# A three-part change in the first projection of a diffusion block: inverse roots by `pow`, later transposes, four modulation vectors made there

## The chip, the cores and the metric

The kernel runs on one core of a Trainium2 chip. The metric is the device time of one execution in microseconds (us). The engines of the core are TensorE (PE; its weight loads are PEld), VectorE (DVE), ScalarE (ACT), GpSimd (POOL) and SyncE (SP), which here only issues DMAs.

## The reference, cut to what matters

Two layers of a transformer with adaptive normalisation run over 256 latent and 256 context tokens of width 1024, all in float32. Each layer has six modulation vectors, `silu(cond) @ ada_w + ada_b`, cut into six parts of 1024 (numbered 0 to 5 here): shift, scale and gate of the mixer, then of the FFN. The first layer is attention plus a convolution and a plain FFN, the second an S5 state-space mixer and a mixture of eight experts.

```
sh1, sc1, g1, sh2, sc2, g2 = adaln(c, ada_w[l], ada_b[l])
h = modulate(rmsnorm(x, norm1_g[l]), sh1, sc1)
q, k, v, a, g = split(h @ w_in)             # 1024 -> 5 x 512
q, k = rmsnorm(heads(q), q_g), rmsnorm(heads(k), k_g)      # per head of 64
u = a * sigmoid(g); u = conv31(u)           # depthwise over tokens
y = concat(attention(q, k, v), silu(layernorm(u))) @ w_out
x = x + g1 * y
x = x + g2 * ffn(modulate(rmsnorm(x, norm2_g[l]), sh2, sc2))
```

`rmsnorm` of q and k needs, for each of 512 tokens and 8 heads, `1 / sqrt(mean of squares + 1e-6)`: 128 partitions by 32 numbers for q, as many for k.

## The kernel before, in words

**Matrix products.** Each float32 weight tile of 128x2048 (1 MB) is loaded into one of four ring buffers `raw`, then split (`split`, L190) into a rounded part `wh` (ScalarE, L203) and a rest `wl` (VectorE, or GpSimd for the names in `ON_POOL`, L205). `mm3` (L221) makes three matmuls of 128x128 by 128x512 for each product (L223 to L225). Splitting a tile frees its ring buffer, and `Stream.issue` then issues the next load. The order of all loads is written out in `plan` (L238) and goes through SP's queue in that order.

**First projection** (`mix_in`, L577). Five outputs n of 512 columns are made in the order 3, 4, 0, 1, 2: conv input a, gate g, q, k, v. Each takes two weight tiles (`kh` 0 and 1), each tile four steps k, each step four token tiles t: 48 matmuls a tile. When q's two tiles are done, ScalarE squares the four accumulators (L655), VectorE sums per head (L656), `rsqrt` (L494) makes the inverse roots by a bit trick and three Newton steps on VectorE, and VectorE writes the normalised `qn` (L658) from the accumulators in PSUM. `rest` is what TensorE then has to do for the last output (for n = 4 the transposes `glu` of a times gate, L592; for q and k the transposes `turn_qk`, L601, whose results ScalarE copies, L602); it is called inside the next output's loop, so those transposes stand between its matmuls.

**Convolution.** After `glu`, 31 taps for each of four channel blocks go into lists (`conv`, L662): VectorE does three blocks (L676), GpSimd one (add, L686, of a product that ScalarE makes, L685, in two buffers). `pump` (L227) takes a few taps of each list per step k (`MIXV`, `MIXP`); what is left goes into the attention.

**Modulation vectors.** The first two of layer 0 are made at the start. Each of the others is four units (`ada_unit`, L364): one 1 MB tile of `ada_w` and four products `ada_mm` (L333) with a 32-column weight, put on four column groups of TensorE. Two units are one half; ScalarE copies its accumulator out (`ada_out`, L371) and issues a store of rows (for vectors 2 to 5 of layer 1 to `partd`, `ada_to_dram`, L430). The units wait in a list in the order of the `ada_queue` calls in `layer0`; `ada_step` (L465) takes up to n of them, if their loads have been issued. Before the change the list begins with layer 0's vectors 2, 3 and 4, taken in the attention (L813), then 0's 5 and 1's 0 to 5, taken two at a time in the FFN loop (L964) and in its tail (`tail`, L854, `TAIL`). `partd` is read at the start of the S5 stage (L1246).

**Order.** Instructions of the engines listed in `ORDERED` are kept in the order of the program; for "mix" (the first projection) these are ScalarE, GpSimd and SP. TensorE and VectorE are ordered there by the compiler's scheduler. PSUM has eight banks of 128x512, all under one tag (L180).

**Later stages.** Attention, output projection, FFN, S5 and at last the experts (`moe`), whose 336 weight tiles are loaded through the ring and through buffers that earlier stages lend once they are done with them.

Of the kernel before, what the change touches and what calls it, by code (L numbers as in the profile page):

```python
# [15 lines left out]
P = 128  # L16
# [140 lines left out]
class Kernel:  # L157
# [80 lines left out]
    def plan(self):  # L238
# [16 lines left out]
        mix(4), mix(0), mix(1), mix(2)  # L255
# [6 lines left out]
        halves = [(l, v, n) for l, v in ((0, 5), (1, 0), (1, 1), (1, 2), (1, 3), (1, 4), (1, 5)) for n in range(2)]  # L262
# [5 lines left out]
        for u in range(11):  # L268
            st.add(("w1", u), a["ffn_w1"][u])
            if u < 9:  # L270
# [9 lines left out]
        half(), half()  # L280
# [28 lines left out]
    def setup(self):  # L309
# [6 lines left out]
        self.mhalf = c.tile([P, 8], F32, name="mhalf")  # L316
# [177 lines left out]
    def rsqrt(self, ss, n, count):  # L494

        V = self.nc.vector
        v, y, t = (self.wk([P, n], name, 1) for name in ("nv", "ny", "nt"))
        V.tensor_scalar(v, ss, 1.0 / count, EPS, op0=OP.mult, op1=OP.add)
        V.tensor_scalar(y.bitcast(I32), v.bitcast(I32), 1, None, op0=OP.logical_shift_right)
        V.tensor_scalar(y.bitcast(I32), y.bitcast(I32), -1, 0x5f3759df, op0=OP.mult, op1=OP.add)  # L500
        V.tensor_scalar(v, v, -0.5, None, op0=OP.mult)
        for _ in range(3):
            V.tensor_tensor(t, y, y, op=OP.mult)
            V.tensor_tensor(t, t, v, op=OP.mult)
            V.scalar_tensor_tensor(y, t, 1.5, y, op0=OP.add, op1=OP.mult)
        return y
# [70 lines left out]
    def mix_in(self, second):  # L577
# [27 lines left out]
        for i, (n, kh) in enumerate(order):  # L605
# [5 lines left out]
            for k in range(4):  # L611
# [12 lines left out]
                if rest and k == 1 and (kh if n else not kh):  # L624
                    rest()
                    rest = None
                if i:
                    self.pump(t=10, v=MIXV[n] if n < 3 else 0, p=MIXP[n] if n < 3 else 0)
# [98 lines left out]
    def attention(self):  # L727
# [79 lines left out]
        for i in range(n + 3):  # L807
# [5 lines left out]
            if i and len(self.vec) < 6:  # L813
# [1366 lines left out]
    def layer0(self):  # L2180
# [5 lines left out]
        gates = lambda: self.gates  # L2186
        self.ada_to_rows(0, 2, gates)
# [5 lines left out]
        for i, v in enumerate((2, 3, 4, 5)):  # L2193
            self.ada_to_dram(1, v, i)
# [85 lines left out]
ADAU = 10  # L2280
# [35 lines left out]
```

## Time and profile before

| | us |
|---|---|
| runs before: median of 3 (lowest to highest) | 1881.32 (1877.25 to 1883.44) |
| the profiled execution's own time | 1882.24 |
| its span in the profile | 1880.5 |
| TensorE busy | 1726.7 (92%) |
| VectorE busy | 1241.2 (66%) |
| ScalarE busy | 811.1 (43%) |
| GpSimd busy | 472.7 (25%) |

The profile is one execution. Times of day in it are us from the start of the span. An arrow in a row names what ended a wait; x16 after a name is the number of instructions in the row. Busy time of TensorE is pipelined, so matmuls that start 0.23 us apart each last 0.39 us.

### The profile page before, as it was taken

The numbers are of one execution on the slowest core, as the hardware profiler recorded it, in microseconds if no ns is written. First come the engines' busy times: TensorE is split into PE (matmuls) and PEld (weight loads), VectorE is DVE, ScalarE is ACT, GpSimd is POOL, SyncE is SP. The second block draws the span as 40 slices with busy tenths as digits, with TensorE's granted clock in tenths as the row PEclk, the third lists the DMA queues.
The fourth block names the chain that finished last, engine by engine and source line by source line (L and its number), as shares of the span: only waits on it lengthen the run. The fifth ranks groups of instructions, "written<-read, shape, count | busy, mean of one in ns | idle before, by whom it ended". The sixth has DMA issues, their size and how long they took to land. (4 is left out here: it accounts for less than half of the span.)

```text
span 1880.5 us, 23867 instructions
## 1 busy us (share of the span) xinstructions
PE 1726.7 (92%) x8730; PEld 1190.5 (63%) x8730; DVE 1241.2 (66%) x1709; ACT 811.1 (43%) x1156; POOL 472.7 (25%) x528
## 2 busy tenths in 40 slices
PE   6977898999979999896689999999999999999996
PEld 3855376876757778674478863578536783368732
DVE  4999797576775654768789951489316973189621
ACT  3434664432332332546357740467205661167500
POOL 2347057395893900245140000000000000000000
PEclk9988999999999999998789999999999999999999
DMA  8320734753645543449668989999899999999897
GB/s 323 129 67 23 272 123 155 253 191 128 222 153 181 188 160 108 159 159 196 253 257 345 372 326 419 420 420 389 339 420 420 419 347 380 419 420 419 316 419 288
DMA packets 107437, 517.08 MB, mean 275 GB/s; under 512 B 13792, under 2 KB 41696, under 8 KB 48688
## 3 DMA queue, kind: packets, MB, share of 16 engines
q1 hardware_dynamic: 76672, 490.77, 68.0%
q10 hardware_dynamic: 29968, 22.57, 3.8%
q0 software_dynamic: 672, 2.14, 0.4%
q8 instruction: 71, 1.16, 0.3%
q14 instruction: 54, 0.44, 0.1%
HBM read 496.46 MB, written 18.97 MB: 274 GB/s over the span
## 5 line engine op out<-in xcount | busy, mean ns | idle before, releaser
L203 ACT CAST wh<-raw 128x1024 fp32r<-128x1024 f32 x192 | 194.8, 1049 | 162.7 <-PE w L225 75.0
L205 DVE TENSOR_TENSOR wl<-raw,wh 128x1024 fp32r<-128x1024 f32 x171 | 215.9, 1298 | 37.7 <-ACT wh L203 37.6
L2020 PE MATMUL m<-raw,E 128*64 128x512 f32 x360 | 166.7, 603 | 4.5 <-DMA raw<-in_moe 4.5
L224 PE MATMUL w<-hl,wh 128*128 128x512 f32 (+1 forms) x384 | 144.0, 375 | 1.2 <-POOL hl L568 0.6
L223 PE MATMUL w<-hh,wh 128*128 128x512 f32 (+1 forms) x384 | 144.9, 378 | 0.0
L225 PE MATMUL w<-hh,wl 128*128 128x512 f32 (+1 forms) x384 | 142.6, 372 | 0.0
L224 PE MATMUL m<-wl,small 128*128 128x512 f32 x336 | 132.6, 395 | 6.9 <-DVE wl L205 6.9
L223 PE MATMUL m<-wh,small 128*128 128x512 f32 x336 | 135.3, 403 | 0.0
L225 PE MATMUL m<-wh,small 128*128 128x512 f32 x336 | 132.4, 394 | 0.0
L1965 DVE SCALAR_TENSOR_TENSOR gt<-lth,m 64x512 f32<-64x512 f32 x28 | 19.0, 680 | 143.4 <-ACT lth L1964 142.9
L1844 POOL TENSOR_SCALAR brow<-pw,order 128x128 fp32r<-128x128 f32 x6 | 4.8, 793 | 355.5 <-PE xT L1868 355.5
L2020 PE MATMUL m<-U,E 128*64 128x512 f32 x184 | 86.0, 608 | 4.9 <-DMA U<-in_moe 4.9
L2020 PEld LDWEIGHTS m<-raw,E 128*64 128x64 f32 x360 | 46.1, 137 | 67.1 <-issue 54.6
L2036 ACT COPY E<-gT 128x256 f32<-128x256 f32 x28 | 10.4, 373 | 178.5 <-PE gT L2034 178.3
L223 PEld LDWEIGHTS w<-hh,wh 128*128 128x128 f32 x384 | 72.4, 189 | 17.0 <-issue 3.4
L2020 PE MATMUL m<-room,E 128*64 128x512 f32 x176 | 80.6, 598 | 2.5 <-DMA room<-in_moe 2.5
L224 PEld LDWEIGHTS w<-hl,wh 128*128 128x128 f32 x384 | 72.6, 189 | 14.9 <-POOL hl L568 2.8
L1844 POOL TENSOR_SCALAR brow<-order 128x128 fp32r<-128x128 f32 x8 | 7.8, 974 | 292.4 <-PE xT L1850 280.9
L224 PE MATMUL w<-wl,gh 128*128 128x512 f32 x176 | 72.1, 410 | 10.0 <-DVE wl L205 10.0
L225 PEld LDWEIGHTS w<-hh,wl 128*128 128x128 f32 x384 | 72.5, 189 | 12.9
L205 POOL TENSOR_TENSOR wl<-raw,wh 128x1024 fp32r<-128x1024 f32 x21 | 53.0, 2536 | 98.5 <-ACT wh L203 98.3
L224 PEld LDWEIGHTS m<-wl,small 128*128 128x128 f32 x336 | 63.9, 190 | 20.3 <-DVE wl L205 7.9
(444 smaller groups left out, 4545.4 us busy)
## 6 DMA issues: line engine op xcount, KB each, us to landing
raw<-in_moe SPq DMA_DIRECT2D x135, 1024.0 KB, 8.8
U<-in_moe SPq DMA_DIRECT2D x67, 1024.0 KB, 13.2
room<-in_moe SPq DMA_DIRECT2D x66, 1024.0 KB, 8.8
raw<-in_ada_w SPq DMA_DIRECT2D x48, 1024.0 KB, 5.2
xres<-in_moe SPq DMA_DIRECT2D x34, 1024.0 KB, 13.3
h<-in_moe SPq DMA_DIRECT2D x34, 1024.0 KB, 12.0
raw<-in_ffn_w SPq DMA_DIRECT2D x30, 1024.0 KB, 4.9
raw<-in_mix_w_in SPq DMA_DIRECT2D x10, 1024.0 KB, 7.9
```

Source lines behind the costliest of these rows:

```text
L203: nc.scalar.copy(wh[:, :m], flat[:, h:h + m])
L205: eng.tensor_tensor(wl[:, :m], flat[:, h:h + m], wh[:, :m].bitcast(F32), op=OP.subtract)
L223: nc.tensor.matmul(o, lhsT=ah, rhs=bh, start=start, stop=False)
L224: nc.tensor.matmul(o, lhsT=ah, rhs=bl, start=False, stop=False)
L225: nc.tensor.matmul(o, lhsT=al, rhs=bh, start=False, stop=stop)
L1844: eng.tensor_scalar(self.perm[:, t], self.iota64 if FEW[e] and not beyond else self.iota, pos, mask, op0=OP.is_equal, op1=OP.mult)
L1965: nc.vector.scalar_tensor_tensor(g[hi], th[lo], 1.0, o[lo], op0=OP.add, op1=OP.mult)
L2020: nc.tensor.matmul(o[64 * i:64 * i + 64], lhsT=self.few[:, 4 * j + k], rhs=w[i][:, k], start=not j and not k, stop=j == 1 and k == 3, tile ...
L2036: nc.scalar.copy(gT, pt[:, 0:256])
```

## The change

The Newton steps of `rsqrt` give way to one `pow` on GpSimd, with the exponent -0.5 in `mhalf`, made wider. `rest` for q and k is called after step k = 3 of the second tile of the next output instead of after k = 1 (for `glu` nothing changes). The sixteen units of layer 1's vectors 2 to 5 are put at the head of the list and taken one at each step k of the second tiles of gate, q, k and v; their loads stand between the tiles of `mix_w_in`, and their slots in the FFN's loads and steps go.

```
--- before.py
+++ after.py
@@ -252,14 +252,19 @@
                 for j in range(2):
                     part(0, v, n, j)
             mi(3, n)
-        mix(4), mix(0), mix(1), mix(2)
+        mi(4, 0)
+        for i, n in enumerate((4, 0, 1, 2)):
+            mi(n, 1)
+            if n != 2:
+                mi((n + 1) % 5, 0)
+            ada(1, 2 + i)
         for qt in range(2):
             st.add(("bias", qt), a["bias"][:, qt])
         ada(0, 2), ada(0, 3), ada(0, 4)
         for kh in (1, 0):
             for n in range(2):
                 st.add(("mo", n, kh), unit(a["mix_w_out"][n], 4 * kh, 4))
-        halves = [(l, v, n) for l, v in ((0, 5), (1, 0), (1, 1), (1, 2), (1, 3), (1, 4), (1, 5)) for n in range(2)]
+        halves = [(l, v, n) for l, v in ((0, 5), (1, 0), (1, 1)) for n in range(2)]
 
         def half():
             l, v, n = halves.pop(0)
@@ -267,7 +272,7 @@
                 part(l, v, n, j)
         for u in range(11):
             st.add(("w1", u), a["ffn_w1"][u])
-            if u < 9:
+            if u < 3:
                 half()
             st.add(("w3", u), a["ffn_w3"][u])
             if u < 3:
@@ -277,7 +282,6 @@
                 for n in range(2):
                     for f in range(lo, hi, 4):
                         st.add(("w2", f, n), unit(a["ffn_w2"][n], f, min(4, hi - f)))
-        half(), half()
         for j in range(2):
             for kh in range(2):
                 st.add(("si", j, kh), a["ssm_w_in"][j, kh].rearrange("p r k f -> p r (k f)"))
@@ -313,7 +317,7 @@
         self.x = c.tile([P, 4, D], F32, name="xres")
         self.cols = c.tile([P, NCOLS], F32, name="cols")
         self.sil = c.tile([P, 8, 32], F32, name="sil")
-        self.mhalf = c.tile([P, 8], F32, name="mhalf")
+        self.mhalf = c.tile([P, 32], F32, name="mhalf")
         self.cnt = c.tile([P, 24], I32, name="cnt")
         cc = self.wk([P, 8, 2], "gt", 2)
         nc.scalar.dma_start(cc, a["cc"])
@@ -493,16 +497,9 @@
 
     def rsqrt(self, ss, n, count):
 
-        V = self.nc.vector
-        v, y, t = (self.wk([P, n], name, 1) for name in ("nv", "ny", "nt"))
-        V.tensor_scalar(v, ss, 1.0 / count, EPS, op0=OP.mult, op1=OP.add)
-        V.tensor_scalar(y.bitcast(I32), v.bitcast(I32), 1, None, op0=OP.logical_shift_right)
-        V.tensor_scalar(y.bitcast(I32), y.bitcast(I32), -1, 0x5f3759df, op0=OP.mult, op1=OP.add)
-        V.tensor_scalar(v, v, -0.5, None, op0=OP.mult)
-        for _ in range(3):
-            V.tensor_tensor(t, y, y, op=OP.mult)
-            V.tensor_tensor(t, t, v, op=OP.mult)
-            V.scalar_tensor_tensor(y, t, 1.5, y, op0=OP.add, op1=OP.mult)
+        v, y = (self.wk([P, n], name, 1) for name in ("nv", "ny"))
+        self.nc.vector.tensor_scalar(v, ss, 1.0 / count, EPS, op0=OP.mult, op1=OP.add)
+        self.nc.gpsimd.tensor_tensor(y, v, self.mhalf[:, :n], op=OP.pow)
         return y
 
     def chain(self, xn, xT, perm=False):
@@ -621,9 +618,11 @@
                             self.split(("mi", 3, 1))
                 if first:
                     first.pop(0)()
-                if rest and k == 1 and (kh if n else not kh):
+                if rest and ((kh, k) == (1, 3) if n else (kh, k) == (0, 1)):
                     rest()
                     rest = None
+                if i > 1 and kh:
+                    self.ada_step(1)
                 if i:
                     self.pump(t=10, v=MIXV[n] if n < 3 else 0, p=MIXP[n] if n < 3 else 0)
             if not i:
@@ -810,7 +809,7 @@
             if i - 2 in soft:
                 pTs[i - 2] = turn_p(soft.pop(i - 2))
             ss = scores(*jobs[i]) if i < n else None
-            if i and len(self.vec) < 6:
+            if i and len(self.vec) < 14:
                 self.ada_step()
             self.pump(v=TAPS[0], p=TAPS[1])
             if ss:
@@ -2184,14 +2183,14 @@
         sh2 = self.const.tile([P, 2, 8, 2], F32, name="shsc2")
         shs = self.const.tile([P, 2, 8, 2], F32, name="shsc3")
         gates = lambda: self.gates
+        for i, v in enumerate((2, 3, 4, 5)):
+            self.ada_to_dram(1, v, i)
         self.ada_to_rows(0, 2, gates)
         for i, v in enumerate((3, 4)):
             self.ada_to_cols(0, v, sh2[:, i], C_AB + 16 + 8 * i)
         self.ada_to_rows(0, 5, gates)
         for i in range(2):
             self.ada_to_cols(1, i, shs[:, i], C_AB + 32 + 8 * i)
-        for i, v in enumerate((2, 3, 4, 5)):
-            self.ada_to_dram(1, v, i)
         with tc.tile_pool(name="l0", bufs=1) as self.l0:
             self.s5_params(self.l0.tile([P, 32, 64], F32, name="room", tag="gates"))
             self.hh, self.hl = self.halves()
@@ -2277,7 +2276,7 @@
 MIXP = (1, 1, 3)
 ADDS = ((0,), (1,), (2,), (3,), (4,), (5,))
 TAIL = (0, 0, 2, 0, 1, 1)
-ADAU = 10
+ADAU = 3
 EARLY = (4, ('si', 0, 0))
 START = ((1, 3), (1, 3), (1, 3), (3, 1))
 SPLIT1 = (2, 3)
```

## Rows read from the trace of the kernel before

**Rows 1.** The page, part 2: busy tenths of PE and of the DMA engines in 40 slices of 47 us.

```profile
PE   6977898999979999896689999999999999999996
...
DMA  8320734753645543449668989999899999999897
```

**Rows 2.** Waits, 85 to 186 us: engine and line, waited for; us in total, times, longest.

```profile
PE qT L601 <- DVE qn L658: 25.0, 2, 12.9
```

**Rows 3.** Stretches: us, then busy us and instructions by engine, granted clock, DMA share, GB/s.

```profile
121.30:134.20 12.90, 0.04 (x2) 0.01 (x1) 12.90 (x20) 1.98 (x3) 7.16 (x4) 0.64 0.00 1
```

**Rows 4.** Groups by line, 60 to 330 us: count | busy us, mean ns | idle before.

```profile
L676 DVE SCALAR_TENSOR_TENSOR cv<-upad,cols,cv 128x512 f32<-128x512 f32 x90 | 70.5, 820 | 0.0
...
L503 DVE TENSOR_TENSOR nt<-ny 128x32 f32<-128x32 f32 x6 | 6.5, 1078 | 0.0
...
L505 DVE SCALAR_TENSOR_TENSOR ny<-nt,ny 128x32 f32<-128x32 f32 x6 | 6.4, 1075 | 0.0
...
L504 DVE TENSOR_TENSOR nt<-nt,nv 128x32 f32<-128x32 f32 x6 | 5.4, 895 | 0.0
...
L491 POOL TENSOR_TENSOR rn<-rv,mhalf 128x1 f32<-128x1 f32 x8 | 4.5, 565 | 71.4 <-DVE rv L490 71.4
...
L499 DVE TENSOR_SCALAR ny<-nv 128x32 int32<-128x32 int32 x2 | 2.6, 1277 | 0.0
```

**Rows 5.** Timeline of DVE: start us, us, instruction.

```profile
115.70 0.17 DVE L498 TENSOR_SCALAR nv<-qss 128x32 f32<-128x32 f32 x1
...
150.57 0.17 DVE L498 TENSOR_SCALAR nv<-qss 128x32 f32<-128x32 f32 x1
...
172.15 2.47 DVE L658 TENSOR_TENSOR qn<-mi,ny 128x512 f32<-128x512 f32 x4
```

**Rows 6.** Timeline of PE in the first projection.

```profile
85.80 1.91 PE L592 MATMUL uT<-ident,aT 128*128 128x128 f32 x16
...
98.23 0.39 PE L225 MATMUL mi<-wh,hl 128*128 128x512 f32 x1
...
103.67 0.39 PE L225 MATMUL mi<-wh,hl 128*128 128x512 f32 x1
...
134.20 4.72 PE L601 MATMUL qT<-ident,qn 128*128 128x128 f32 x16 [12.86 <-DVE qn L658]
```

**Rows 7.** Timeline of PE in the tail of the FFN.

```profile
770.75 1.92 PE L334 MATMUL ada<-raw,sil 128*32 128x512 f32 x16
...
779.67 1.06 PE L334 MATMUL ada<-raw,sil 128*32 128x512 f32 x8
```

**Rows 8.** Waits, 395 to 800 us.

```profile
ACT wh L203 <- PE w L225: 75.0, 14, 11.5
...
PE w L224 <- DVE wl L205: 10.0, 2, 5.5
```

**Rows 9.** Timeline of POOL in the first projection.

```profile
150.93 27.17 POOL L686 TENSOR_TENSOR cv<-cv,ptap 128x512 f32<-128x512 f32 x15 [3.15 <-ACT ptap L685]
...
179.19 1.29 POOL L686 TENSOR_TENSOR cv<-cv,ptap 128x512 f32<-128x512 f32 x1 [1.09 <-ACT ptap L685]
```

**Rows 10.** Timeline of ScalarE, end of the first projection and start of the attention.

```profile
145.69 1.07 ACT L655 ACTIVATE gt<-mi 128x512 f32<-128x512 f32 x2
...
175.36 1.37 ACT L602 ACTIVATE qk<-qT,cols 128x512 f32<-128x512 f32 x2
...
182.14 2.62 ACT L648 COPY v<-mi 128x512 f32<-128x512 f32 x4 [3.10 <-PE mi L225]
...
186.96 0.48 ACT L767 ACTIVATE prob<-S,nm 128x256 f32<-128x256 f32 x1 [2.19 <-DVE nm L760]
...
190.98 1.05 ACTq L417 DMA_DIRECT2D gated<-adsb  x1
```

**Rows 11.** Copies of the modulation's sums, 395 to 800 us: ns min/median/max, first and last start.

```profile
L373 ACT COPY adsb<-ada x8: 586/589/597, 467.9 to 784.2; 128x512 f32<-128x512 f32 x8
```

**Rows 12.** The page, part 6: DMA issues, KB each, us to landing.

```profile
raw<-in_mix_w_in SPq DMA_DIRECT2D x10, 1024.0 KB, 7.9
```

More of the change, by code (lines that the diff above doesn't have):

```diff
@@ L254, in plan @@
             mi(3, n)
-        mix(4), mix(0), mix(1), mix(2)
+        mi(4, 0)
+        for i, n in enumerate((4, 0, 1, 2)):
+            mi(n, 1)
+            if n != 2:
+                mi((n + 1) % 5, 0)
+            ada(1, 2 + i)
         for qt in range(2):
@@ L261, in plan @@
                 st.add(("mo", n, kh), unit(a["mix_w_out"][n], 4 * kh, 4))
-        halves = [(l, v, n) for l, v in ((0, 5), (1, 0), (1, 1), (1, 2), (1, 3), (1, 4), (1, 5)) for n in range(2)]
+        halves = [(l, v, n) for l, v in ((0, 5), (1, 0), (1, 1)) for n in range(2)]
         def half():
@@ L269, in plan @@
             st.add(("w1", u), a["ffn_w1"][u])
-            if u < 9:
+            if u < 3:
                 half()
@@ L279, in plan @@
                         st.add(("w2", f, n), unit(a["ffn_w2"][n], f, min(4, hi - f)))
-        half(), half()
         for j in range(2):
@@ L315, in setup @@
         self.sil = c.tile([P, 8, 32], F32, name="sil")
-        self.mhalf = c.tile([P, 8], F32, name="mhalf")
+        self.mhalf = c.tile([P, 32], F32, name="mhalf")
         self.cnt = c.tile([P, 24], I32, name="cnt")
@@ L494, in rsqrt @@
     def rsqrt(self, ss, n, count):
[L496 to L505, printed above, removed]
+        v, y = (self.wk([P, n], name, 1) for name in ("nv", "ny"))
+        self.nc.vector.tensor_scalar(v, ss, 1.0 / count, EPS, op0=OP.mult, op1=OP.add)
+        self.nc.gpsimd.tensor_tensor(y, v, self.mhalf[:, :n], op=OP.pow)
         return y
@@ L623, in mix_in @@
                     first.pop(0)()
-                if rest and k == 1 and (kh if n else not kh):
+                if rest and ((kh, k) == (1, 3) if n else (kh, k) == (0, 1)):
                     rest()
                     rest = None
+                if i > 1 and kh:
+                    self.ada_step(1)
                 if i:
@@ L812, in attention @@
             ss = scores(*jobs[i]) if i < n else None
-            if i and len(self.vec) < 6:
+            if i and len(self.vec) < 14:
                 self.ada_step()
@@ L2186, in layer0 @@
         gates = lambda: self.gates
+        for i, v in enumerate((2, 3, 4, 5)):
+            self.ada_to_dram(1, v, i)
         self.ada_to_rows(0, 2, gates)
@@ L2192, in layer0 @@
             self.ada_to_cols(1, i, shs[:, i], C_AB + 32 + 8 * i)
-        for i, v in enumerate((2, 3, 4, 5)):
-            self.ada_to_dram(1, v, i)
         with tc.tile_pool(name="l0", bufs=1) as self.l0:
@@ L2279 @@
 TAIL = (0, 0, 2, 0, 1, 1)
-ADAU = 10
+ADAU = 3
 EARLY = (4, ('si', 0, 0))
```

## The prediction

> **What bounds the kernel now.** I began with the slices of the page: PE is near full in most of the span, but the third and fourth (94 to 188 us) show 7 tenths, and from the 22nd (987 us) on the DMA row is near full [rows 1]. So the last 890 us, the experts, are bound by their loads; those can start only when the stages before have freed buffers, so time saved earlier shifts all of it. Then I asked for the waits of the first projection, 85 to 186 us. The reader is to see one wait that counts: PE stands 25.0 us, in two pieces, at the transposes of q and k, until DVE has written the normalised qn [rows 2]. The stretch view shows such a piece: for 12.9 us PE is all but idle while DVE is busy throughout, and the granted clock falls to 0.64 [rows 3]. The groups and the DVE timeline say what DVE does: the Newton steps of `rsqrt`, twelve tiny 128x32 instructions per tensor, most of them over 1 us and each followed by a convolution tap, so that 21.6 us lie between the mean of k and its qn [rows 4, 5]. After the wait the 16 transposes take 4.72 us, where 16 like them before took 1.91 [rows 6]. In the FFN it is the other way round: ScalarE waits 75.0 us there for PE to free weight buffers [rows 8], so PE sets the pace, and what it need not do is gained.
>
> **Newton steps out.** L499 and L500 (alike), L501 (not shown, a fill of 128x32 like L498, 0.17) and three rounds of L503 to L505 go: 2 x 2.6 + 0.3 + 6.5 + 5.4 + 6.4 = 23.8 us of DVE for both tensors, and with them the taps between [rows 4, 5]. In comes one `pow` of 128x32 on POOL per tensor. The trace has `pow` only as 128x1, at 0.565 us [rows 4]. A bound from below is that same 0.57; from above, 32 columns one after the other, 32 x 0.565 = 18.1 us. Nothing lies between, so I take their geometric mean, 3.2 us. A larger `mhalf` costs a memset at the start, beside loads: nothing, 1 us if it were in the way.
>
> **Sixteen units of modulation moved.** A pair of units takes PE 1.92 us [rows 7], so 0.96 each. The eight copies between 467.9 and 784.2 stand for 16 units, two to a copy [rows 11]; four of these units are in the tail [rows 7], so six pairs go out of the FFN's main loop: 6 x 1.92 = 11.5 us of PE at its bound. Of the four in the tail the first pair, at 770.75, stands ahead of matmuls that DVE awaits, the other two, one by one from 779.67, between transposes that follow DVE's pace [rows 7]; I count 0.8 us. The copies, 0.59 us each, and their row stores leave ScalarE's queue there too; they had PE as cover, so nothing.
>
> In the projection four units go into each second half-tile of gate, q, k and v. Twenty-four matmuls are 5.44 us (98.23 to 103.67), so a half-tile of 48 is 10.9 [rows 6] and one with units 14.7. *Gate:* its second half ends at 85.80 - 5.44 = 80.4 now, at 84.2 then. ScalarE must copy the last unit before the tanh, but DVE's older work hides most of that; the transposes `uT` and all taps start 3.8 us later. *q:* DVE's taps are the bound from there to the mean of q, now 115.7, then 119.5 [rows 5]; qn can follow 3.2 us later, by about 125. PE comes to q's transposes, now after the fourth k step, at 84.2 + 10.9 + 1.9 + 14.7 + 10.9 + 10.9 + 2.9 = 136.4, so the wait of 12.9 is gone, with the slow transposes behind it. Half-tile q/k ends near 139 rather than 134.2 + 4.7 + 5.4 = 144.3: 5 us ahead. *k:* what is late next? On ScalarE the copies of k's transposes stand behind the products for the POOL taps (15 of them now; 16 then, since the transposes move past one more). These wait for POOL, which runs 15 taps in 27.17 us, 1.81 each, and that is already why the copies came at 175.36, three us after qn began at 172.15 [rows 5, 9, 10]. So removing k's wait gives only what POOL's chain allows. Its start: the squares move from 145.69 to 139.3 + 0.6 + 1.05 + 0.7 = 141.6, behind the last unit's copy, its store and a product, the mean of k from 150.57 to 146.5 [rows 5, 10], `pow` ends at 149.7, and POOL's taps are queued behind it. Fourteen must end before the sixteenth product: 25.3 us at 1.81, or 18.1 at 1.29, the tap at 179.19, which began with POOL idle [rows 9]. DVE has 16 taps of 0.82, some 13 us, beside this [rows 4], about half, so I take the middle, 21.7: 171.4. Then 0.7 for the product, 4 x 0.69 copies, 0.59 and up to 1.05 for the last unit's copy and store, 2.62 for v: exp begins at 179.1 where it began at 186.96 [rows 10, 11], a gain of 7.9 (4.3 to 11.5 with the two tap times).
>
> The rows show small DVE instructions between 0.17 and 1.28 us, and POOL taps between 1.29 and 1.81. The Trainium skill, SBUF — State Buffer, section Who interferes with whom, says that a VectorE instruction with two inputs in SBUF and a reading GpSimd instruction exclude one another for the whole instruction. The trace agrees in kind; by that rule alone the taps would fall to 1.29 once DVE is quiet, and the sum would be nearer its upper end, 11.5.
>
> *Loads:* SP now carries 16 MB between the projection's tiles, past the two bias tiles and the units of the attention. With four buffers each tile of weights is issued when a unit of the half-tile before last is done, over 20 us before its use; landing takes 7.9 [rows 12] and the split some 4. Bias is issued near 154 and used after 178. So nothing; if a landing did show, up to 7.9 per tile. PE must find PSUM banks: q's (k's) accumulators hold four until qn is written, so the first unit of the next second half waits for `pow`: at q, from 119.5 + 3.2 + 0.7 = 123.4, needed at 122.4 + 2.7 = 125.1. It passes by 1.7 us.
>
> **Sum.** 7.9 + 11.5 + 0.8 = 20.2 us. The profiled execution took 1882.24 us (span 1880.5), 0.9 above the median of the three runs, 1881.32. 1882.2 - 20.2 = **1862.0**.
>
> **Rivals.** *A, `pow` counts its columns.* If half of the 0.57 is per column, 0.28 x 32 = 9 us. Then POOL's chain starts 5.8 later and PE waits 9 - 4.9 = 4.1 at the bank: 20.2 - 9.9 = 10.3, 1872. For it: no POOL row here does a transcendental cheaply; against: POOL's plain 128x512 taps show that columns can be much cheaper than a start. Chance 0.16. *B, slower: `pow` at its upper bound.* At 18.1 the PE wait comes back through the bank (18.1 - 4.9 = 13.2) and the chain starts 14.9 later: 20.2 - 28.1 = -7.9, 1890. The sign turns where (p - 3.2) + (p - 4.9) = 20.2, at 14.2 us. Chance 0.06. *C, the FFN gives nothing back:* DVE and ScalarE jobs of the tables take PE's place as bound there; two PE waits on DVE, 10.0 us together, show that they can; the 75 us that ScalarE waits speak against [rows 8]. 1882.2 - 7.9 = 1874; 0.08. *D, more:* taps at 1.29 and `pow` at 0.57 give 7.9 + 3.6 + 2.6 + 12.3 = 26.4, 1856; 0.08. *E, it does not do what it says:* a unit's step does nothing if its load has not been issued, or the scheduler, which orders PE and DVE in this stage by its own estimate, puts qn behind taps and keeps the wait: the projection then loses 16 x 0.96 = 15.4 and the FFN gains 12.3, 1885, or about level where half of it hides; 0.06. The forecast itself: 0.56.
>
> **Numbers.** A measurement of this kernel tells 0.3%, 5.6 us, from no change. The forecast, A, C and D lie below 1875.7; a part of C and E may fall within. So faster 0.86, same 0.08, slower 0.06. The range runs from D, a little lowered for a clock that no longer falls, to between A and C: 1853 to 1873.
>
> **What would show it.** Right: the wait of PE on qn gone from the list; DVE without 128x32 steps; `pow` near 3 us; the 16 transposes of q at about 2 us; exp of the attention near 179; ScalarE's copies of k's transposes still held by POOL's taps; only 12 units in the FFN and that stage about 11 us shorter. Wrong: `pow` over 9 us, PE waiting at the units of the projection (for banks or loads), or an FFN as long as before.

## The result: 1.0% slower, 1899.9 us where 1862 was forecast

| us | before | after |
|---|---|---|
| median of 4 runs each (lowest to highest) | 1881.94 (1877.25 to 1883.44) | 1899.87 (1897.84 to 1902.95) |
| span of the profiled execution | 1880.5 | 1897.0 |
| start of the first exponential of the attention | 186.96 | 212.53 |
| last matmul of the output projection | 313.5 | 340.4 |
| last `w` matmul of the FFN | 776.1 | 792.8 |

The ratio is 1.0103, with a 95% interval of 1.0083 to 1.0124. The three last lines say where to look. The first projection lost 25.6 us and the attention with the output projection 1.3 more; the FFN, from 313.5 to 776.1 before, went from 462.6 to 452.4 and gave 10.2 back; behind it the distance stays (16.7, then 16.5 at the end of the span). So the FFN's half of the forecast came, and the projection, which was to give 7.9, took 25.6.

**Profile after.** The page's part 2 shows PE and DMA by slices of 47 us and answers to [rows 1]: the third and fourth slice of PE are fuller, the fifth is emptier, and the moved loads stand in the second to fourth slice of the DMA row.

```profile
PE   6988689998998999897589999999999999999997
...
DMA  8445462583344343247877989999899998999797
```

The waits of the first projection, 85 to 212 us, answer to [rows 2]: engine and line, waited for; us in total, times, longest.

```profile
ACT adsb L377 <- PE ada L338: 24.0, 5, 9.0
...
DVE qn L657 <- POOL ny L502: 10.7, 2, 5.3
...
PE qT L598 <- ACT adsb L377: 8.8, 1, 8.8
...
PE ada L338 <- DVE qn L657: 6.6, 2, 4.4
```

TensorE's 25.0 us wait for qn is gone, as forecast. In its place stand VectorE at the `pow` (twice 5.34), the units of modulation at the bank that qn holds, and k's transposes behind a unit's copy.

The groups by line, 60 to 330 us, answer to [rows 4]:

```profile
L675 DVE SCALAR_TENSOR_TENSOR cv<-upad,cols,cv 128x512 f32<-128x512 f32 x90 | 86.1, 1026 | 0.0
...
L502 POOL TENSOR_TENSOR ny<-nv,mhalf 128x32 f32<-128x32 f32 x2 | 12.7, 6358 | 13.4 <-DVE nv L501 13.4
```

A `pow` of 128x32 takes 6.36 us, twice the value taken. And the same 90 taps of VectorE that took 70.5 us now take 86.1: of the 23.8 us of Newton steps that went, 15.6 came back as longer taps. (In kernel 6 below, where the steps go and nothing else changes, the 90 taps take 88.7 us.)

VectorE's timeline answers to [rows 5] (start us, us, instruction, count; L501 is the mean of squares, L657 qn, L759 the first maxima of the attention):

```profile
107.21 18.43 DVE L675 SCALAR_TENSOR_TENSOR cv<-upad,cols,cv 128x512 f32<-128x512 f32 x23
125.56 1.27 DVE L655 TENSOR_REDUCE qss<-gt 128x8 f32<-128x512 f32 x2
...
129.73 0.17 DVE L501 TENSOR_SCALAR nv<-qss 128x32 f32<-128x32 f32 x1
...
136.37 2.48 DVE L657 TENSOR_TENSOR qn<-mi,ny 128x512 f32<-128x512 f32 x4 [5.34 <-POOL ny L502]
...
142.67 23.19 DVE L675 SCALAR_TENSOR_TENSOR cv<-upad,cols,cv 128x512 f32<-128x512 f32 x27
...
169.95 0.17 DVE L501 TENSOR_SCALAR nv<-qss 128x32 f32<-128x32 f32 x1
...
176.59 2.49 DVE L657 TENSOR_TENSOR qn<-mi,ny 128x512 f32<-128x512 f32 x4 [5.34 <-POOL ny L502]
179.00 32.90 DVE L675 SCALAR_TENSOR_TENSOR cv<-upad,cols,cv 128x512 f32<-128x512 f32 x28
211.82 1.28 DVE L759 TENSOR_REDUCE nm<-S 128x2 f32<-128x512 f32 x2
```

The reader is to see three blocks of taps in the way: 23 ahead of q's sums (34 taps in all stand ahead of them, 22 before), 27 ahead of k's, 28 ahead of the attention's maxima. The mean of k came at 150.57 before and comes at 169.95, 19.4 later; from there to the first maxima there were 35.7 us (150.57 to 186.24) and are 41.9. The two, 19.4 and 6.2, are the 25.6 us.

TensorE's timeline answers to [rows 6], ScalarE's to [rows 10]:

```profile
86.08 1.07 PE L338 MATMUL ada<-raw,sil 128*32 128x512 f32 x8 [1.59 <-DMA raw<-in_ada_w]
...
92.77 1.91 PE L589 MATMUL uT<-ident,aT 128*128 128x128 f32 x16
...
102.97 1.06 PE L338 MATMUL ada<-raw,sil 128*32 128x512 f32 x8
...
106.95 1.06 PE L338 MATMUL ada<-raw,sil 128*32 128x512 f32 x8
...
137.12 1.94 PE L338 MATMUL ada<-raw,sil 128*32 128x512 f32 x8 [4.43 <-DVE qn L657]
...
151.09 2.03 PE L598 MATMUL qT<-ident,qn 128*128 128x128 f32 x16
```

```profile
116.05 0.59 ACT L377 COPY adsb<-ada 128x512 f32<-128x512 f32 x1 [5.48 <-PE ada L338]
...
117.83 1.06 ACT L654 ACTIVATE gt<-mi 128x512 f32<-128x512 f32 x2
...
155.96 1.06 ACT L654 ACTIVATE gt<-mi 128x512 f32<-128x512 f32 x2
...
200.12 2.56 ACT L599 ACTIVATE qk<-qT,cols 128x512 f32<-128x512 f32 x4
...
205.03 2.06 ACT L647 COPY v<-mi 128x512 f32<-128x512 f32 x4 [0.56 <-ACT adsb L377]
212.53 0.47 ACT L766 ACTIVATE prob<-S,nm 128x256 f32<-128x256 f32 x1 [5.45 <-DVE nm L759]
```

A step k with a unit lasts 3.98 us (102.97 to 106.95), one without 5.44 / 2 = 2.72 [rows 6], so a unit is 1.26 us there, not 0.96. q's transposes take 2.03 us without a wait, at a granted clock of 1.00 (the 2.4 GHz level); the 4.72 us of before followed 12.9 us of idling and had 0.53, close to the 1.2 GHz level. The squares of q start at 117.83, 15.8 us later than the 102.06 of before: gate is 7.0 us late, three units (3.8 us) stand ahead of the end of q's products, and on ScalarE the squares stand behind the copy and the store of the fourth unit (116.05). ScalarE's copies of k's transposes stand behind the products for GpSimd's taps, as forecast (200.12, before 175.36 [rows 10]). GpSimd (to [rows 9]) runs its taps behind k's `pow`:

```profile
156.20 10.79 POOL L685 TENSOR_TENSOR cv<-cv,ptap 128x512 f32<-128x512 f32 x1 [6.13 <-ACT ptap L684]
170.20 6.36 POOL L502 TENSOR_TENSOR ny<-nv,mhalf 128x32 f32<-128x32 f32 x1 [3.22 <-DVE nv L501]
176.53 26.20 POOL L685 TENSOR_TENSOR cv<-cv,ptap 128x512 f32<-128x512 f32 x16
```

### The profile page after: what moved, and what is told of

It is laid out like the page before. It is cut to its first block, busy times and chain, and to the rows that moved or that the text cites. A ratio compares the mean times of both kernels' runs of the same rounds, so it can differ in the third digit from the quotient of the medians.

```text
span 1897.0 us, 23836 instructions
## 1 busy us (share of the span) xinstructions
PE 1748.8 (92%) x8730; PEld 1188.8 (63%) x8730; DVE 1244.9 (66%) x1685; ACT 808.5 (43%) x1156; POOL 489.0 (26%) x530
## 5 line engine op out<-in xcount | busy, mean ns | idle before, releaser
L205 DVE TENSOR_TENSOR wl<-raw,wh 128x1024 fp32r<-128x1024 f32 x171 | 221.6, 1332 | 36.3 <-ACT wh L203 34.6
L675 DVE SCALAR_TENSOR_TENSOR cv<-upad,cols,cv 128x512 f32<-128x512 f32 x90 | 86.1, 1026 | 0.0
L2035 ACT COPY E<-gT 128x256 f32<-128x256 f32 x28 | 10.4, 372 | 175.6 <-PE gT L2033 175.6
L224 PE MATMUL w<-wl,gh 128*128 128x512 f32 x176 | 70.5, 401 | 10.4 <-DVE wl L205 10.4
## 6 DMA issues: line engine op xcount, KB each, us to landing
U<-in_moe SPq DMA_DIRECT2D x67, 1024.0 KB, 10.6
room<-in_moe SPq DMA_DIRECT2D x66, 1024.0 KB, 10.4
xres<-in_moe SPq DMA_DIRECT2D x34, 1024.0 KB, 10.4
raw<-in_mix_w_in SPq DMA_DIRECT2D x10, 1024.0 KB, 10.2
```

What stands on the lines that cost most here:

```text
L205: eng.tensor_tensor(wl[:, :m], flat[:, h:h + m], wh[:, :m].bitcast(F32), op=OP.subtract)
L224: nc.tensor.matmul(o, lhsT=ah, rhs=bl, start=False, stop=False)
L675: nc.vector.scalar_tensor_tensor(o, u, w(cb, k), o, op0=OP.mult, op1=OP.add)
L2035: nc.scalar.copy(gT, pt[:, 0:256])
```

## The experiments

Each line is one kernel: its ratio to the runs of before on the same chip (their medians lie between 1879.3 and 1881.9) with its 95% interval; and from the profile of one execution, in us, the mean of k, the first exponential, the last matmul of the output projection, and the FFN from there to its last `w` matmul.

| kernel | median us | ratio (95%) | mean of k | first exp | output proj. | FFN |
|---|---|---|---|---|---|---|
| before | 1881.9 | | 150.6 | 187.0 | 313.5 | 462.6 |
| after | 1899.9 | 1.0103 (1.0083 to 1.0124) | 170.0 | 212.5 | 340.4 | 452.4 |
| 1 units alone | 1889.9 | 1.0069 (1.0032 to 1.0107) | 168.2 | 206.5 | 331.0 | 454.6 |
| 2 `pow` alone | 1889.5 | 1.0058 (1.0039 to 1.0078) | 151.8 | 194.0 | 317.5 | 460.5 |
| 3 later transposes alone | 1882.7 | 1.0012 (1.0001 to 1.0024) | 152.1 | 185.8 | 312.6 | 462.2 |
| 4 `pow` and later transposes | 1893.5 | 1.0076 (1.0053 to 1.0099) | 156.3 | 195.4 | 321.3 | 460.8 |
| 5 `pow` of k twice | 1897.5 | 1.0095 (1.0074 to 1.0116) | 151.7 | 199.4 | 326.5 | 460.4 |
| 6 root on ScalarE alone | 1882.8 | 1.0016 (1.0002 to 1.0031) | 146.8 | 184.0 | 309.8 | 460.1 |
| 7 GpSimd's taps elsewhere | 1883.6 | 1.0009 (0.9993 to 1.0025) | 166.3 | 188.7 | 315.9 | 462.4 |
| 8 4 with fewer taps | 1899.5 | 1.0119 (1.0083 to 1.0155) | 155.7 | 188.9 | 325.8 | 459.5 |
| 9 root on ScalarE, fewer taps | 1887.2 | 1.0040 (1.0025 to 1.0054) | 150.3 | 177.6 | 319.3 | 459.5 |
| 10 units in the attention | 1930.3 | 1.0268 (1.0239 to 1.0297) | | 185.8 | 366.5 | 454.4 |
| 11 all, VectorE in order | 1895.4 | 1.0081 (1.0059 to 1.0103) | 159.1 | 201.5 | 330.4 | 458.0 |
| 12 units, VectorE in order | 1886.9 | 1.0049 (1.0029 to 1.0069) | 158.9 | 199.3 | 323.7 | 452.2 |
| 13 12, attention in order too | 1914.9 | 1.0180 (1.0157 to 1.0203) | 161.5 | 201.2 | 354.3 | 452.8 |
| 14 control: before, in order as 13 | 1916.7 | 1.0195 (1.0172 to 1.0217) | 156.9 | 192.3 | 349.8 | 462.8 |
| 15 4, taps ahead, in order as 13 | 1928.7 | 1.0255 (1.0234 to 1.0276) | 175.2 | 198.3 | 358.0 | 458.7 |
| 16 root on ScalarE, later, in order as 12 | 1890.2 | 1.0053 (1.0034 to 1.0073) | 154.8 | 189.4 | 318.9 | 462.7 |

The profiled executions took within 2.2 us of their kernel's median, except that of 12: 1881.3, which is 5.6 below.

### The parts by themselves (1 to 4, 11)

*1, units alone:* the change with `rsqrt` and the call of `rest` as before.

```
-                if rest and ((kh, k) == (1, 3) if n else (kh, k) == (0, 1)):
+                if rest and k == 1 and (kh if n else not kh):
...
-        self.nc.gpsimd.tensor_tensor(y, v, self.mhalf[:, :n], op=OP.pow)
+        for _ in range(3):
+            V.tensor_tensor(t, y, y, op=OP.mult)
...
```

> Only the sixteen units moved into the projection; Newton steps and the early transposes as before. Theory 'order' (the compiler's scheduler sees PE later by the units and puts 12 more convolution taps ahead of q's sums on VectorE, 34 instead of 22): about 1895 us, slower by some 13, with the start of the first exp of the attention 20 us or more later than 187 and the FFN about 10 us shorter. Theory 'pow' (the 6.36 us instruction on GpSimd, twice, with its queue, is what costs): no pow here, so about 1878 to 1884, level with the kernel before.

*2, `pow` alone:* `rsqrt` and `mhalf` of the change, all else as before.

```
-        V.tensor_scalar(y.bitcast(I32), v.bitcast(I32), 1, None, op0=OP.logical_shift_right)
...
+        self.nc.gpsimd.tensor_tensor(y, v, self.mhalf[:, :n], op=OP.pow)
```

> Only the pow, with the transposes and the units as before. Theory 'order': the order ahead of q's sums is that of before (22 taps), pow of 6.4 us replaces 16.5 us of Newton steps and taps, so 3 to 8 us faster, 1874 to 1879; first exp near 181. Theory 'pow': 5 us or more slower, 1887 or more.

*3, later transposes alone:* the condition of `rest` of the change, all else as before.

```
-                if rest and k == 1 and (kh if n else not kh):
+                if rest and ((kh, k) == (1, 3) if n else (kh, k) == (0, 1)):
```

> The Newton steps of before with the later transposes alone (the four vectors stay in the feed-forward part). Theory CHAIN (the stage ends by the mean of k, then what makes k's factors, then GpSimd's taps and the copies behind them; q's wait is beside that chain): TensorE's 25.0 us wait for q's factors shrinks to below 15, the first exponential moves by less than 2 us either way from 186.96, and the time is that of before within 4 us. Theory WAIT (my prediction's: what TensorE idles for q's factors is the stage's own time): the first exponential comes 8 to 12 us earlier, and the time is 1868 to 1873 beside 1880 of before.

*4,* the edits of 2 and 3 together.

> The pow and the later transposes, without the units. Theory 'order': PE's two waits at the transposes nearly gone, first exp bound by GpSimd's taps and by 23 taps of VectorE near 181, total 1873 to 1879. Theory 'pow': slower than 1885. If the moved units are what costs 27 us in the projection, this run is the one without them and without their gain of 9.4 us in the FFN.

*11, the whole change, with VectorE kept in the order of the program in the first projection:*

```
-    "mix": ("Activation", "Pool", "SP"),
+    "mix": ("DVE", "Activation", "Pool", "SP"),
```

> The whole change, and VectorE kept in the order of the program in the first projection, so that 21 taps stand ahead of q's sums instead of 34. Theory 'order': first exp near 187 to 192 instead of 212.5, total about 1872 to 1877, faster than both. Theory 'pow', and a theory 'ScalarE' (its queue waits 30 us for units): still over 1892.

What follows: each part is slower by itself, or no faster. The units cost 0.69%, the `pow` 0.58%, the later transposes 0.12%; together 1.39% where the change has 1.03%, so they overlap in part. At the first exponential the units alone cost 19.6 us, the `pow` 7.1, and the later transposes gain 1.2; together 25.5, where the change lost 25.6. (That this fits so closely is in part luck: 2 and 3 together, in 4, lose 8.5.) The idea that the scheduler's order alone was to blame falls here: in the order of the program the first exponential comes only 11.0 us earlier (212.5 to 201.5) and the time falls by a fifth of the loss, and the `pow` costs without any units. The transposes speak to another point. TensorE's wait for qn is shorter in 3 (21.0 us between 100 and 215 us, 25.0 before; below 15 was expected), and the first exponential moved by 1.2 us. In 4 the same edit takes 10.6 us off that wait (18.4 in 2, 7.8 in 4), and the first exponential comes 1.4 us later. So that wait stood beside the chain that sets the end, not on it.

### The `pow` (5, 8)

*5:* 2 with the `pow` of k done a second time, to the same result.

```
...
-        self.nc.gpsimd.tensor_tensor(y, v, self.mhalf[:, :n], op=OP.pow)
+        for _ in range(times):
+            self.nc.gpsimd.tensor_tensor(y, v, self.mhalf[:, :n], op=OP.pow)
...
```

> The kernel with the power operation alone (1889.5, first exponential at 194.0), in which the power operation of k is done twice. Theory CHAIN: it lies with its 6.4 us between the mean of k and GpSimd's fifteen taps, so the first exponential comes 5 to 7 us later, at 199 to 201, and the time is 1894 to 1897. Theory ORDER (the order in which VectorE's taps were put sets the end, and GpSimd's operation is beside it): first exponential within 1.5 us of 194.0, time 1888 to 1891.

The timelines of VectorE and GpSimd in 5:

```profile
163.81 0.69 DVE L652 TENSOR_TENSOR qn<-mi,ny 128x512 f32<-128x512 f32 x1 [10.85 <-POOL ny L499]
...
172.76 25.98 DVE L670 SCALAR_TENSOR_TENSOR cv<-upad,cols,cv 128x512 f32<-128x512 f32 x23
198.68 1.27 DVE L754 TENSOR_REDUCE nm<-S 128x2 f32<-128x512 f32 x2
```

```profile
151.90 11.87 POOL L499 TENSOR_TENSOR ny<-nv,mhalf 128x32 f32<-128x32 f32 x2 [3.04 <-DVE nv L497]
163.74 24.78 POOL L680 TENSOR_TENSOR cv<-cv,ptap 128x512 f32<-128x512 f32 x15
```

VectorE's wait grows from 5.34 us in 2 to 10.85, and the first exponential comes 5.4 us later (194.0 to 199.4). The second `pow` took 5.5 (11.87 less 6.36). So the `pow` of k is on the chain with its whole price. Two queues stand behind it. On VectorE qn was put straight behind the mean, and taps that were ready wait behind qn. On GpSimd, in order, the taps wait.

*8:* 4 with fewer taps given out in the last third of the projection.

```
-MIXV = (3, 3, 2)
-MIXP = (1, 1, 3)
+MIXV = (3, 3, 0)
+MIXP = (1, 1, 1)
```

> The power operation with the later transposes (1893.5, first exponential at 195.4), with no VectorE taps and 1 GpSimd tap in place of 2 and 3 given out for each step of the last third of the projection; the taps left over go to the attention. Theory TAPS (what the Newton steps left free on VectorE was filled with taps of the convolution that stand ahead of the attention's maxima, and GpSimd's own taps stand behind the power operation; the price of 6.4 us itself is hidden or small): the first exponential comes at 178 to 186, and the time is 1873 to 1881. Theory PRICE (what the power operation takes is on the path to the scores whatever the taps do): first exponential at 193 or later, time 1890 or more. If the taps left over lengthen the attention by as much, the first exponential is early and the end of the output product is not before 313.

The first exponential came 6.5 us earlier than in 4, not the 9 to 17 expected: 23 taps still stood between k's qn and the maxima (164.73, 23.55 us), older ones. And the attention with the output projection became longer by more (125.9 in 4, 136.9 here). Taps put off are not taps saved.

*15:* 4 with GpSimd's taps given out earlier, and VectorE in the order of the program in both stages.

```
-MIXP = (1, 1, 3)
+MIXP = (2, 3, 3)
...
-    "mix": ("Activation", "Pool", "SP"),
-    "attention": ("SP",),
+    "mix": ("DVE", "Activation", "Pool", "SP"),
+    "attention": ("DVE", "SP"),
```

> The power operation and the later transposes, the four vectors in the feed-forward part, GpSimd given 2 taps for 1 in the first two thirds of the projection, so that few are queued behind the power operation of k, and VectorE kept in the order of the program in the projection and in the attention. Theory CHAIN: nothing of 26 us stands behind the second power operation, so the copies of k's transposes come 15 us or more earlier than with the power operation and the later transposes together, and the first exponential comes at 175 to 185 beside 195.4; the time is 1872 to 1882. Theory PRICE (the power operation costs what it takes, 6.4 us twice, wherever GpSimd's taps are): first exponential 192 to 197, time 1890 to 1895.

At 1.0255 it tells little of the `pow`: 14, below, shows that this order of VectorE costs 1.95% by itself.

### What the Newton steps cost (7, 6, 9)

*7:* before, with no GpSimd taps given out in the projection.

```
-MIXP = (1, 1, 3)
+MIXP = (0, 0, 0)
```

> The kernel before, with no GpSimd taps given out in the projection (all 31 go to the attention); the work is the same. Theory SHARE (the Newton steps took 1.0 to 1.3 us each because GpSimd's taps ran beside them, and VectorE's taps take up that time when the steps are taken out): the 22 steps take below 0.3 us each, VectorE's taps 0.70 to 0.76 us, from the mean of k to its factors' first use there are 10 to 14 us in place of 21.6 with as many taps between, and the first exponential comes at 165 to 178; the attention is 8 to 25 us longer for its taps. Theory OWN (a step takes above 1 us because each reads what the one ahead of it wrote): steps above 0.9 us, first exponential above 183.

It went another way than written: the scheduler, free to order GpSimd's work of the attention, put those taps ahead, between 90 and 148 us. That makes a better test than the one meant: in one execution q's steps run beside GpSimd's taps and k's do not. GpSimd, then VectorE at q, then VectorE at k:

```profile
89.95 34.46 POOL L686 TENSOR_TENSOR cv<-cv,ptap 128x512 f32<-128x512 f32 x20 [1.73 <-ACT ptap L685]
...
130.14 17.55 POOL L686 TENSOR_TENSOR cv<-cv,ptap 128x512 f32<-128x512 f32 x9 [1.88 <-ACT ptap L685]
```

```profile
108.07 16.89 DVE L676 SCALAR_TENSOR_TENSOR cv<-upad,cols,cv 128x512 f32<-128x512 f32 x10
...
135.44 1.27 DVE L503 TENSOR_TENSOR nt<-ny 128x32 f32<-128x32 f32 x1
136.63 0.74 DVE L676 SCALAR_TENSOR_TENSOR cv<-upad,cols,cv 128x512 f32<-128x512 f32 x1
137.29 1.28 DVE L504 TENSOR_TENSOR nt<-nt,nv 128x32 f32<-128x32 f32 x1
...
154.85 7.37 DVE L676 SCALAR_TENSOR_TENSOR cv<-upad,cols,cv 128x512 f32<-128x512 f32 x11
...
169.11 0.18 DVE L503 TENSOR_TENSOR nt<-ny 128x32 f32<-128x32 f32 x1
169.21 0.74 DVE L676 SCALAR_TENSOR_TENSOR cv<-upad,cols,cv 128x512 f32<-128x512 f32 x1
169.88 0.18 DVE L504 TENSOR_TENSOR nt<-nt,nv 128x32 f32<-128x32 f32 x1
```

The same instruction, in the same alternation with taps, takes 1.27 us beside GpSimd and 0.18 without it. What ends a slow step can be read beside GpSimd's own taps:

```profile
134.81 1.84 POOL L686 TENSOR_TENSOR cv<-cv,ptap 128x512 f32<-128x512 f32 x1
...
136.73 1.78 POOL L686 TENSOR_TENSOR cv<-cv,ptap 128x512 f32<-128x512 f32 x1
```

These two taps end at 136.65 and 138.51, the two slow steps above at 136.71 and 138.57. In the kernel before it is the same: all 17 steps of over 1 us end 0.04 to 0.05 us behind a GpSimd instruction, and the 9 quick instructions of the same size have less than 0.1 us beside one. The steps' own work is some 22 x 0.18 = 4 us of the 23.8 (an estimate from these rows); the rest is waiting for GpSimd's instructions to end. A VectorE tap behind another pays in the same way: ten take 16.89 us beside GpSimd's taps, eleven 7.37 without. This is what the Trainium skill, SBUF — State Buffer, section Who interferes with whom, says of a VectorE instruction with two inputs in SBUF and a reading GpSimd instruction; its rule that the one blocks the other for the whole instruction fits these rows in kind. The first two steps of q, with one input, are as slow (1.25 and 1.26 us). The third, with one as well, took 0.17, but it falls where GpSimd goes from one tap to the next (134.69, with the taps changing at 134.74 to 134.81), so it doesn't show that such a step is spared.

*6:* before, with another way to the root that has neither steps nor GpSimd.

```
-        V.tensor_scalar(y.bitcast(I32), v.bitcast(I32), 1, None, op0=OP.logical_shift_right)
...
+        self.nc.scalar.activation(y, v, AF.Sqrt)
+        self.nc.vector.reciprocal(y, y)
```

> The kernel before with ScalarE's square root and VectorE's reciprocal in place of the Newton steps, and nothing else. Theory SHARE (VectorE gains only what the 22 steps take beside GpSimd's taps less what its own taps then take there, and nothing 6.4 us long stands between the mean and the factors): first exponential at 181 to 186, time 1875 to 1881, so the same as before or a little faster, 8 to 14 us below the power operation alone. Theory STEPS (the 23.8 us of the Newton steps are to be won once the power operation's price is gone): first exponential at 165 to 175, time 1857 to 1868.

```profile
146.76 0.17 DVE L497 TENSOR_SCALAR nv<-qss 128x32 f32<-128x32 f32 x1
...
155.96 27.39 DVE L670 SCALAR_TENSOR_TENSOR cv<-upad,cols,cv 128x512 f32<-128x512 f32 x22
183.27 1.28 DVE L754 TENSOR_REDUCE nm<-S 128x2 f32<-128x512 f32 x2
```

This is the answer to what the steps were worth. With them out and no 6.4 us in their place, the mean of k comes 3.8 us earlier and the first exponential 3.0 earlier; the time is 0.16% longer (0.02 to 0.31), so nothing is gained. From the mean of k to the maxima there are 36.5 us (before 35.7) with 26 taps there in place of 24. Put side by side, that stretch is 35.7 with the steps, 36.5 with the root on ScalarE, 41.5 with the `pow` (151.79 to 193.33), 47.0 with it twice, 41.9 in the change (28 taps in each of these three), and 38.5 in 4 (23 taps): the steps cost nothing there, the first `pow` some 5 us, with two taps more than in 6, and a second 5.5.

One thing stays open. In its profile 6 was 6.2 us ahead of before at the last `w` matmul of the FFN, and 0.7 ahead at the end of the span; from the first to the last `m` matmul of the experts there are 873.2 us, and 869.9 before. With one execution of each, no run tells whether the experts swallow such a lead or only scatter by as much (868.6 in 14). So "time saved earlier shifts all of it", on which the prediction rests, was not shown for a gain of this size.

*9:* 6 with the edits of 3 and 8.

> The root on ScalarE and VectorE with the later transposes, VectorE in the scheduler's order, and the taps of the last third given out as in the run with fewer taps. Theory TAPS: like that run, and without the 6.4 us before the factors of k, so the first exponential is 3 to 7 us earlier than there, at 174 to 182, and the time 1869 to 1878. Theory PRICE: the first exponential is 10 us or more earlier than with the power operation and fewer taps.

It has the earliest exponential of all, 9.4 us ahead of before, and still the output projection ends 5.8 later: the attention, 126.6 us before from the first exponential to that end, became 141.7. It is 11.3 us ahead of 8, as the theory of the price had it (10 or more).

*16:* 6 with the edit of 3 and VectorE in the order of the program in the projection (the edit of 11).

> As the power operation with the later transposes, but the inverse root is made by ScalarE's square root and VectorE's reciprocal, with VectorE in the order of the program in the projection: nothing of it is on GpSimd, so that GpSimd's taps are free to begin with ScalarE's products as in the kernel before. Theory CHAIN: GpSimd's taps begin at 148 to 154 as before, and the first exponential comes at 180 to 187; the time is 1872 to 1881. Theory PRICE: as good as without the power operation's 6.4 us twice, first exponential 182 to 184 from 195.4, time 1880 to 1883. Against both: ScalarE's in-order queue, which holds copies of q and k behind the square root; then the first exponential comes at 190 or later and the time is 1885 or more.

GpSimd's taps began at 157.87 there, and k's copies behind them at 182.24; the first exponential at 189.4 is between what the theories had, nearer to that of ScalarE's queue, and so is the time (1890.2, where that theory had 1885 or more). It is 6.0 us ahead of 4, about what the `pow` takes, though the order differs; against 14, below, which has the steps and the same order, it is 2.9 ahead, as 6 is 3.0 ahead of before.

### The units (10, 12, 13, 14)

*10:* before, with the four vectors made in the attention; their loads stand ahead of the output projection's.

```
...
-            if i and len(self.vec) < 6:
+            if i and len(self.vec) < 14:
...
```

> The kernel before with its Newton steps and its early transposes; only the four vectors are made in the attention in place of the feed-forward part, one half at each job, and their weights are loaded ahead of the output product's. Theory PLACE (the feed-forward part gives about 10 us back whenever the vectors leave it, and the loss of the change is from where they were put): projection as before (first exponential at 185 to 189), output product ended 2 to 8 us later than 313.5, feed-forward part 451 to 455 from 462.6, time 1872 to 1880. Rival (the eight halves cost as much wherever they are): output product ended 10 us or more later, time 1880 to 1888.

The FFN gives 8.2 us here too, so that gain follows the units out of it. But the way from the first exponential to the end of the output projection becomes 54 us longer, and the time of 1930.3 lies far beyond both theories (1872 to 1888). TensorE waits there at 15 of the 28 units for their loads, 26.4 us in all; what makes up the rest of the 54 is not shown.

```profile
ACT adsb L374 <- PE ada L335: 52.1, 12, 7.3
...
PE ada L335 <- DMA raw<-in_ada_w: 26.4, 15, 2.7
```

*13 and its control 14:* 1 and before, both with VectorE in the order of the program in projection and attention (the last four lines of 15's edit).

> The four vectors in the projection with the Newton steps (1889.9 with VectorE in the scheduler's order, first exponential at 206.5), with VectorE in the order of the program in the projection and the attention. Theory ORDER (the 85 taps that stand ahead of the first exponential, in place of 67, are what the units cost; TensorE's 20 us of units go into its waits for the factors): first exponential at 187 to 196, time 1872 to 1882. Theory TENSORE (a unit of 1.26 us costs its own time, 16 of them 20 us, whatever VectorE's order): first exponential at 202 or later, time 1886 or more.

> The control of the run above: the kernel before with VectorE in the order of the program in the projection and the attention, nothing else. Theory ORDER: within 5 us of before, 1876 to 1885, since there the scheduler's order did not put more taps ahead. If the order of the program is worse by itself (the scheduler fills the gaps between Newton steps with taps, the program puts the steps one behind the other), the time is 1888 or more and the run above is to be read against this one.

*12:* 1 with VectorE in that order in the projection alone (the edit of 11).

> The four vectors in the projection with the Newton steps, VectorE in the order of the program in the projection alone (the attention's order by itself cost about 35 us). Theory ORDER: first exponential at 195 to 202 in place of 206.5, the output product ended 4 to 11 us before 331.0, feed-forward part 452 to 455, time 1879 to 1886. Theory TENSORE: first exponential at 204 or later, time 1888 or more.

The order costs 1.95% by itself, most of it in the attention, so 13 has to be read against 14: there the units put the first exponential 8.9 us back (192.3 to 201.2), where in the scheduler's order it was 19.6; the output projection ends 4.5 later, the FFN gives 10.0, and the two medians differ by 1.8 us the other way. In 12 the output projection ends 7.3 us earlier than in 1, though with 12's median 1886.9 it stays slower than before. 12 has no control of its own, but up to the first exponential 14 can serve as one: it keeps the same order in the projection, and 12 comes 7.0 us behind it (192.3, 199.3).

How the order costs can be seen in 1, at q. VectorE, GpSimd and ScalarE there:

```profile
108.10 15.31 DVE L682 SCALAR_TENSOR_TENSOR cv<-upad,cols,cv 128x512 f32<-128x512 f32 x23
...
125.84 1.28 DVE L662 TENSOR_REDUCE qss<-gt 128x8 f32<-128x512 f32 x2 [2.43 <-ACT gt L661]
```

```profile
111.86 12.71 POOL L692 TENSOR_TENSOR cv<-cv,ptap 128x512 f32<-128x512 f32 x1 [6.04 <-ACT ptap L691]
```

```profile
124.60 0.72 ACT L691 ACTIVATE ptap<-upad,cols 128x512 f32<-128x512 f32 x1 [6.27 <-POOL cv L692]
```

TensorE is later by the units, and the scheduler fills the time with taps: 34 stand ahead of q's sums, 22 before. While 23 of them run, one single tap of GpSimd lasts 12.71 us; ScalarE, whose order is kept, stands 6.27 us at the next product for GpSimd, and q's squares behind it start at 125.23. VectorE, done with its taps, then waits 2.43 us for them. In 12, with 21 taps ahead of the sums, the squares start at 119.21.

So in the scheduler's order the units cost 19.6 us at the first exponential and in the order of the program 7.0 to 8.9: more than half of the cost hangs on how the scheduler puts VectorE's taps. That the rest is TensorE's own time, of the 20 us that 16 units of 1.26 us take, is argued and not shown.

No kernel was faster than before. Those that came nearest (3, 6, 7) leave the four vectors in the FFN and have no `pow`.

## Why the prediction was wrong, step by step

The step that failed is the term of 7.9 us for the projection, which took 25.6 instead. Two assumptions carried it: that of the units only gate's 3.8 us would be felt there, and that the Newton steps were 23.8 us of VectorE's own work. By size the first is the worse: the units alone cost 19.6 us at the first exponential (1), the `pow` alone 7.1 (2).

- **Gate: 3.8 us late, and no other unit was to reach the mean of q; gate alone was 7.0 late** (`uT` from 85.80 to 92.77). A unit is 1.26 us there and not 0.96; one of the four waited 1.59 for its load, where "nothing" was counted; and ScalarE's copy and store of the last unit stand ahead of the tanh.
- **q: "DVE's taps are the bound from there to the mean of q", 119.5.** It was 129.73. The squares, behind q's own units and their copies, start 15.8 us later than before, and the scheduler filled that time with 12 more taps ahead of the sums, which again waited for taps: the squares start at 117.83, the sums at 125.56. The forecast let neither reach the mean.
- **k: the mean at 146.5, exp at 179.1.** It was 169.95 and 212.53. The squares start at 155.96, 14.4 us later than forecast: q's 10.2 and the 3.2 by which the `pow` was dearer are most of it. Then 27 taps stand ahead of the sums: from the squares to the mean there are 14.0 us, 4.9 in the forecast. Last, the sum lets the exponential begin at the end of v's copy. Before, it began 2.2 us behind that end, waiting for the maxima [rows 10], which the sum left out; in the change it is 5.4 (205.03 and 2.06, then 212.53), since 28 taps stand ahead of the maxima.
- **Newton steps out: a gain that was not there.** "2 x 2.6 + 0.3 + 6.5 + 5.4 + 6.4 = 23.8 us of DVE" was read as the steps' own time. In the same place stood 0.17 us for L498 and 1.28 for L499, both of 128x32; the difference was noted, and a rule for it named, but used for GpSimd's taps alone. Kernel 7 shows that the steps are 0.18 us without GpSimd's taps, 6 that taking them out moves the first exponential by 3.0 us and gives nothing at the end. What takes up the time is the 90 taps, 70.5 us before, 88.7 in 6, 86.1 in the change.
- **The price of `pow`: mis-sized.** It was taken as 3.2 us, between 0.57 and 18.1; 6.36 was measured, and at k it is on the path with its whole length (5). Rival A had the kind of cost, at 9 us, but inside a gain that was not there. With the price fell "it passes by 1.7 us" (1.9 by the prediction's own terms, which give 122.6 and not 122.4): the first unit of k's second half waited 4.43 us for the bank.
- **The wait of 12.9: gone, and worth nothing.** q's transposes take 2.03 us without a wait, as forecast (about 2). But what is late next was named only in part. GpSimd's chain was named; that VectorE's taps stand ahead of the attention's maxima was not, and in the change that is what the first exponential waits for (5.45 us).
- **FFN: 12.3 us; it was 10.2.** This was right in kind: the FFN gave 8.0 to 10.4 in 1, 10, 12 and 13, though 4.6 in 11.
- **The rivals.** The clause of E that the scheduler puts work behind taps held in kind, at the sums and the maxima and not at qn, but E gave it 0.06 and 1885. B, the slower one, needed a `pow` of over 14.2 us. None reached 1899.9: A to D start from the 7.9 us of the projection and change a price or another term, and E's loss there is TensorE's 15.4 us alone.

Open: how much of the units' cost in the projection is waiting for loads, how 12 stands at its end to a control in its own order, and what the experts make of a lead of a few us; none was tried.

## What to carry to other kernels

The duration that a profile gives for a small instruction can be another engine's time: before counting it as a gain, find the same shape at a moment when the neighbour is idle, and count only that. Where an engine is full because a list of background work fills every gap, removing work from it only moves that list; what counts is how much of the list stands ahead of the instruction that opens the next stage. And work moved from a stage is worth what it frees there less what it delays where it lands, down to the order that a scheduler then chooses.

## What the hardware showed that was not expected

- `pow` on GpSimd: 0.565 us for 128x1 [rows 4], 6.36 for 128x32, 11.87 for two in a row. From the first two an estimate of (6.36 - 0.565) / 31 = 0.19 us for each further column follows, where an add of 128x512 (x1 at 175.57 in kernel 6) takes 1.27.
- A 128x32 instruction of VectorE takes 0.17 to 0.18 us with GpSimd quiet and mostly 1.24 to 1.29 beside GpSimd's taps, ending 0.04 to 0.05 us behind the end of one. Taps of VectorE in a row come every 0.67 us with GpSimd quiet and every 1.69 beside its taps.
- It works both ways: one GpSimd tap, otherwise mostly 1.3 to 1.8 us, took 10.79 while VectorE ran taps one behind the other (156.20 in the change), and 12.71 in kernel 1.
- Through a buffer this reaches a third engine: in kernel 1 ScalarE stood 6.27 us for that GpSimd tap.
